# One 512-column pass for hi and lo of h, and a weight sum by transfer, in the seven-product units of a streaming encoder layer

## The chip, the cores and the metric

The kernel runs on one core of a Trainium2 chip. The metric is the device time of one execution in microseconds (us); lower is better. PE is the matrix engine (TensorE), DVE is VectorE, ACT is ScalarE, POOL is GpSimd, SP is the engine whose queue issues most transfers.

## The reference

One layer of a hybrid encoder on 512 tokens of width 2048, in float32:

```python
h = rms_norm(x, norm_gains[l, 0])
blocks = jnp.split(h @ w_in[l], 11, axis=-1)      # four head groups work on these
...
mixed = jnp.concatenate([y_sb, y_df, y_lru, y_sc], axis=-1) @ w_out[l]
x = x + rms_norm(mixed, norm_gains[l, 1])
h = rms_norm(x, norm_gains[l, 2])
x = x + rms_norm(conv_geglu_ffn(h, ffn_w_up[l], ffn_conv_w[l], ffn_w_down[l]), norm_gains[l, 3])

def conv_geglu_ffn(h, w_up, conv_w, w_down):
    u = causal_dwconv(h @ w_up, conv_w)           # 3 taps along the tokens
    g, up = jnp.split(u, 2, axis=-1)              # 4096 columns each
    return (jax.nn.gelu(g, approximate=True) * up) @ w_down
```

The change lies in `h @ w_up` and in the step between `@ w_out` and it.

## The kernel before

**Number format.** Each float32 operand of a matmul is split into two parts in PE's fast float32 format: hi (a cast on ScalarE) and lo (what is left, a subtraction on VectorE). A product is three passes: hi x hi, hi x lo and lo x hi. So each 128x128 block of weights has a hi and a lo part, and each block of h has a hi and a lo part that lie apart in one tile.

**Order.** PE's queue is in the order in which the program text issues its matmuls. Work beside the main stream of matmuls (norms, the small matmuls between) is put in by `at(block, fn)`: `tick()` counts half blocks of the stream, and `fn` is issued when its count comes. The other engines' queues are ordered at build time by a scheduler, by readiness and priority; `tc.high_priority` lifts a step, and the taps of the convolution are not lifted.

**After `@ w_out`.** The 512 tokens are worked in two halves. `residual(hf)` (line 827) normalizes the mixed result of a half, adds it to x by four accumulating transfers (POOL queue, 512 KB each, SBUF to SBUF), and books `squares` at 22, 25, 28 and 31 ticks later and `norm2` at 37 ticks later (line 838). `squares` adds up the squares of x on VectorE. `norm2` (line 854) sums them over the partitions with four small matmuls on PE (line 859), makes 1/rms, and scales and splits h. For the second half it also makes the sums of h for the units (`sums_of_h`). The matmuls of `@ w_out`, and then of the first four column tiles of `@ w_up` (`up_plain`), run on in the meantime.

**The units.** The other 28 column tiles of each half of `@ w_up` are done in 28 units (`up_unit`, line 990). A unit has four weight blocks a11, a12, a21, a22 (128 x 1024 numbers each, 512 KB) for two row halves of h and the two halves (gate and value) of the output, and computes the 2x2 block product with seven products instead of eight, from sums of blocks: s3 = a11 + a21, s1 = a21 + a22, s2 = a11 + s1, s4 = a12 + s2. s1 is added in place by an accumulating transfer from HBM on the POOL queue (in the first unit, unit 4, by VectorE); s3, s2 and s4 are added on VectorE (`add`, line 1007). s4 takes the place of a12, whose tile (`w_raw`) is the same buffer in every unit. `raw` (line 995) loads a block on the SP queue, `operand` (lines 1001 and 1002) splits one into hi and lo; three pairs of buffers go round among the operands.

`product` (line 1009) runs one of the seven: for 8 blocks k two matmuls of 256 columns with the weights' hi part (line 1021 with hi of h, line 1022 with lo of h), then 8 matmuls with the weights' lo part (line 1026), all into columns 0 to 255 of one bank. The order is 11, 21, T2, T1, T3, 22, T4; 11, T2, T3 and T4 add up in bank x, T1 and 22 in bank y, 21 is in bank w. After each, `keep` (a copy on ScalarE, line 1041) or `add_result` (an add on VectorE, line 1031) takes the bank's sum out to the tile `ub` (ug and uv in the code), and the next product into that bank waits for it. `add_rest` adds columns 256 to 511 of the bank for the products named in `JOINED`, which is empty. `conv` (lines 941 to 946) and `glu` (line 951) finish the tile, and the result goes to HBM for the down projection.

Of the kernel before, what the change touches and what calls it, by code (L numbers as in the profile page):

```python
# [12 lines left out]
ALU = mybir.AluOpType  # L13
# [3 lines left out]
P = 128  # L17
# [3 lines left out]
FF = 2 * D  # L21
EPS = 1e-6
AHEAD = 1000000

JOINED = ()
ALL = slice(0, S)
HALVES = (slice(0, S // 2), slice(S // 2, S))
NEG = -1e30
# [22 lines left out]
def trunk(ctx: ExitStack, tc: tile.TileContext, xT, params, consts, wgate, w_in, w_out, w_up0, w_up, w_dn, out):  # L51
# [722 lines left out]
    with ExitStack() as ph:  # L774
# [52 lines left out]
        def residual(hf):  # L827

            ts = HALVES[hf]
            ss1[hf].rstd(rstd1[:, ts])  # L830
            acc = ph2.tile([P, 2, S // 2], F32, name="s2")
            for q in range(4):
                for i in range(2):
                    m = mg[q][hf][:, 2 * i:2 * i + 2]
                    V.tensor_tensor(out=m, in0=m, in1=repeated(rstd1[:, ts], 2), op=ALU.mult)
                G.dma_start(out=xs[q][hf], in_=mg[q][hf], accum_op=ALU.add)
                at(clock[0] + 22 + 3 * q, lambda q=q: squares(hf, q, acc))
            at(clock[0] + 37, lambda: norm2(hf, acc))

        def squares(hf, q, acc):  # L840

# [145 lines left out]
        def by4(t):  # L987
            return flat(t).rearrange("p (a b) -> p a b", a=4)

        def up_unit(unit):  # L990
# [14 lines left out]
            def add(out, a, b):  # L1005
                with tc.high_priority(offset=AHEAD):
                    V.tensor_tensor(out=out, in0=a, in1=b, op=ALU.add)

            def product(ps, ops, name, first):


                hi, lo = ops
                kw = {} if first else {"skip_group_check": True}
                own = ps[:, 0:256]
                for k in range(8):
                    w, t = hi[:, k * P:(k + 1) * P], tops[name][k]
                    start = first and k == 0
                    if name in JOINED:
                        T.matmul(ps.rearrange("p (a t) -> p a t", a=2), lhsT=w, rhs=t, start=start, stop=False, **kw)
                    else:  # L1020
                        T.matmul(own, lhsT=w, rhs=t[:, 0], start=start, stop=False, **kw)  # L1021
                        T.matmul(own, lhsT=w, rhs=t[:, 1], start=False, stop=False, **kw)  # L1022
                    if k % 2 == 1:
                        tick()
                for k in range(8):
                    T.matmul(own, lhsT=lo[:, k * P:(k + 1) * P], rhs=tops[name][k][:, 0], start=False, stop=k == 7,  # L1026
                             **kw)

            def add_result(t, ps, *names):
                with tc.high_priority(offset=AHEAD):  # L1030
                    V.tensor_tensor(out=t, in0=t, in1=ps[:, 0:256], op=ALU.add)
                add_rest(t, ps, *names)

            def add_rest(t, ps, *names):
                if any(n in JOINED for n in names):
                    with tc.high_priority(offset=AHEAD):
                        V.tensor_tensor(out=t, in0=t, in1=ps[:, 256:512], op=ALU.add)

            def keep(t, ps, *names):
                with tc.high_priority(offset=AHEAD):  # L1040
                    A.copy(out=t, in_=ps[:, 0:256])
                add_rest(t, ps, *names)

            ug, uv = up_tile(), up_tile()
            lo_, hi_ = slice(2, 258), slice(258, 514)
# [4 lines left out]

            a11, a21 = raw(spare[n], 0, 0), raw(spare[2 + n], 1, 0)
            s3, a12, a22 = (by4(wp.tile([P, 2, S], F32, name="w_raw")) for _ in range(3))
            add(s3, a11, a21)
            s1 = a21
            if unit == 4:
                raw(a22, 1, 1)
                add(a21, a21, a22)
            else:
                with tc.high_priority(offset=AHEAD):
# [7 lines left out]
            keep(ug[:, lo_], x, "11")  # L1067
# [4 lines left out]
            add_result(ug[:, lo_], w, "21")  # L1072
            o1 = operand(s1)
            product(x, o2, "T2", False)
            keep(ug[:, hi_], x, "11", "T2")
# [4 lines left out]
            keep(uv[:, hi_], y, "T1")  # L1080
            o4 = operand(s4)
            product(x, o3, "T3", False)
            add_result(uv[:, hi_], x, "11", "T2", "T3")
            o22 = operand(a22)
            product(y, o4, "22", False)
            add_result(ug[:, hi_], y, "T1", "22")
            gate = conv(ug, 0, unit)
            product(x, o22, "T4", False)
            keep(uv[:, lo_], x, "11", "T2", "T3", "T4")
            glu(unit, gate, conv(uv, 1, unit, minus=True))  # L1090

        for unit in range(4, FF // P):
# [168 lines left out]
```

## Time and profile before

| | |
|---|---|
| median of 3 runs (range) | 1818.74 us (1817.76 to 1820.98) |
| the profiled execution | 1819.11 us |
| its span, first to last instruction | 1817.4 us |
| granted PE clock, mean over the span | 0.99 |
| PE busy | 1770.5 us, 97% of the span |
| DVE busy | 1157.0 us, 64% |
| ACT busy | 875.2 us, 48% |
| POOL busy | 103.1 us, 6% |
| moved by transfers | 256.38 MB, 141 GB/s over the span |

Busy times are sums over the span. PE's matmuls are pipelined, so their durations overlap: what one costs in a stream is read from start to start, not from its duration. A wait in a row stands in brackets: the idle time of the engine ahead of the instruction, and what ended it. The granted clock is the share of PE's full clock (2.4 GHz) that was granted; its lower level is 0.50.

### The profile page before, as it was taken

The page shows a single profiled execution, that of the slowest core. Times are in us where ns is not written, and L with a number is a line of the kernel's source. Part 1 is how long each engine was busy: PE and PEld are TensorE (multiplying, and loading weights), DVE is VectorE, ACT ScalarE, POOL GpSimd, SP SyncE. Part 2 cuts the span into 40 slices and gives each one's busy share as a digit, 9 for nine tenths or more (in the row PEclk, how much of TensorE's full clock was granted, in tenths as well). Part 3 has the DMA queues.
Part 4 walks back from the last instruction along what each step waited for, and adds up shares of the span by engine and source line. Part 5 has one row for each costly group of instructions (what it writes and reads, how often), then busy time and mean ns, then how long its engine had stood idle before and what let it go on. Part 6 is the DMA issues. An engine that isn't in the chain of part 4 may idle for free.

```text
span 1817.4 us, 27666 instructions
## 1 busy us (share of the span) xinstructions
PE 1770.5 (97%) x11180; PEld 1606.3 (88%) x11180; DVE 1157.0 (64%) x1575; ACT 875.2 (48%) x1301; POOL 103.1 (6%) x160
## 2 busy tenths in 40 slices
PE   8999999999999999899899999999999999999995
PEld 6778788887888889889899999999999988888995
DVE  7884576665666235669888887888788752222364
ACT  6442676555344334767555555554555642221342
POOL 0000111100000111100000000000000000010101
PEclk9999999999999999999999999999999999999998
DMA  7234222343332536785655455454544573323465
GB/s 255 82 104 140 75 76 83 100 126 93 93 93 93 196 117 176 230 239 167 189 148 152 140 145 153 138 141 144 156 135 128 181 248 101 97 93 102 130 207 175
DMA packets 83927, 256.38 MB, mean 141 GB/s; under 512 B 9012, under 2 KB 13364, under 8 KB 83800
## 3 DMA queue, kind: packets, MB, share of 16 engines
q1 hardware_dynamic: 78184, 235.23, 40.6%
q0 software_dynamic: 5040, 18.35, 6.1%
q8 instruction: 87, 1.43, 0.3%
q10 hardware_dynamic: 576, 1.05, 0.2%
q14 instruction: 40, 0.33, 0.1%
HBM read 230.47 MB, written 21.24 MB: 139 GB/s over the span
## 4 chain that ended last, share of the span: by engine, by line
PE 88%; DMA 4%; DVE 3%; issue 3%; ACT 2%; POOL 0%; SPq 0%; ACTq 0%; DVEq 0%; POOLq 0%
PE mm L152 39%; PE mm L1021 10%; PE mm L1022 10%; PE mm L1026 10%; PE pa L152 9%; PE mm L123 2%; PE mm L125 2%; PE mm L124 2%; PE pa L577 1%; DMA w_raw<-in_w_up_dram 1%; DMA mg<-in_w_up_dram 1%; DMA xs<-mg 1%; DMA w_raw<-in_w_out_dram 1%; DVE vd L269 1%; ACT w_hi L101 1%
## 5 line engine op out<-in xcount | busy, mean ns | idle before, releaser
L102 DVE TENSOR_TENSOR w_lo<-w_raw,w_hi 128x1024 fp32r<-128x1024 f32 (+1 forms) x249 | 305.1, 1226 | 397.2 <-PE mm L152 187.0
L101 ACT CAST w_hi<-w_raw 128x1024 fp32r<-128x1024 f32 (+1 forms) x249 | 260.6, 1047 | 444.3 <-PE mm L152 289.5
L152 PE MATMUL mm<-a,w_hi 128*128 128x512 f32 (+1 forms) x2048 | 433.1, 362 | 2.8 <-DVE t L320 2.1
L152 PEld LDWEIGHTS mm<-a,w_hi 128*128 128x128 f32 x2048 | 347.8, 190 | 61.2 <-DVE t L320 2.6
L152 PE MATMUL mm<-a,w_lo 128*128 128x512 f32 (+1 forms) x1024 | 230.8, 364 | 0.0
L1021 PE MATMUL mm<-a,w_hi 128*128 128x256 f32 x896 | 221.3, 284 | 5.1 <-ACT w_hi L1001 3.6
L1022 PE MATMUL mm<-a,w_hi 128*128 128x256 f32 x896 | 221.2, 284 | 0.0
L1001 ACT CAST w_hi<-w_raw 128x1024 fp32r<-128x1024 f32 x112 | 117.7, 1051 | 174.4 <-PE mm L1022 142.8
L152 PEld LDWEIGHTS mm<-a,w_lo 128*128 128x128 f32 x1024 | 173.1, 190 | 28.0 <-issue 1.5
L1021 PEld LDWEIGHTS mm<-a,w_hi 128*128 128x128 f32 x896 | 173.0, 193 | 5.6 <-ACT w_hi L1001 3.8
L1022 PEld LDWEIGHTS mm<-a,w_hi 128*128 128x128 f32 x896 | 173.0, 193 | 0.0
L1002 DVE TENSOR_TENSOR w_lo<-w_raw,w_hi 128x1024 fp32r<-128x1024 f32 x112 | 136.7, 1221 | 41.2 <-ACT w_hi L1001 38.7
L1026 PE MATMUL mm<-a,w_lo 128*128 128x256 f32 x896 | 126.0, 283 | 0.2 <-DVE w_lo L1002 0.2
L1001 ACT CAST w_hi<-mg 128x1024 fp32r<-128x1024 f32 x84 | 87.9, 1047 | 75.9 <-PE mm L1022 75.2
L1026 PEld LDWEIGHTS mm<-a,w_lo 128*128 128x128 f32 x896 | 115.8, 192 | 0.4 <-DVE w_lo L1002 0.4
L152 PE MATMUL pa<-a,w_hi 128*128 128x256 f32 (+1 forms) x704 | 108.5, 308 | 5.9 <-ACT w_hi L101 5.9
L1021 PE MATMUL mm<-xs,w_hi 128*128 128x256 f32 x448 | 109.9, 283 | 0.0
L1022 PE MATMUL mm<-xs,w_hi 128*128 128x256 f32 x448 | 109.9, 283 | 0.0
L152 PEld LDWEIGHTS pa<-a,w_hi 128*128 128x128 f32 x704 | 98.6, 197 | 11.7 <-ACT w_hi L101 6.6
L1002 DVE TENSOR_TENSOR w_lo<-mg,w_hi 128x1024 fp32r<-128x1024 f32 x84 | 102.4, 1219 | 3.2 <-ACT w_hi L1001 2.2
L1021 PEld LDWEIGHTS mm<-xs,w_hi 128*128 128x128 f32 x448 | 86.0, 192 | 0.0
L1022 PEld LDWEIGHTS mm<-xs,w_hi 128*128 128x128 f32 x448 | 86.0, 192 | 0.0
(273 smaller groups left out, 2730.5 us busy)
## 6 DMA issues: line engine op xcount, KB each, us to landing
w_raw<-in_w_up_dram SPq DMA_DIRECT2D x88, 512.0 KB, 5.2
w_raw<-in_w_in_dram SPq DMA_DIRECT2D x87, 512.0 KB, 3.6
w_raw<-in_w_dn_dram SPq DMA_DIRECT2D x80, 512.0 KB, 3.7
mg<-in_w_up_dram SPq DMA_DIRECT2D x56, 512.0 KB, 3.7
w_raw<-in_w_out_dram SPq DMA_DIRECT2D x48, 512.0 KB, 3.7
mg<-in_w_up_dram POOLq DMA_DIRECT2D x27, 512.0 KB, 5.8
g_d<-f SPq DMA_DIRECT2D x32, 256.0 KB, 3.0
ys<-g_d SPq DMA_DIRECT2D x32, 256.0 KB, 4.1
```

The lines of the kernel that those rows point to most:

```text
L101: w_split.append(A.copy(out=hi[:, sl], in_=raw[:, sl]))
L102: V.tensor_tensor(out=lo[:, sl], in0=raw[:, sl], in1=hi[:, sl].bitcast(F32), op=ALU.subtract)
L123: T.matmul(ps, lhsT=sh, rhs=mh, start=first, stop=False)
L124: T.matmul(ps, lhsT=sh, rhs=ml, start=False, stop=False)
L125: T.matmul(ps, lhsT=sl, rhs=mh, start=False, stop=last)
L152: T.matmul(pss[u], lhsT=a, rhs=b, start=c == 0 and kk == 0 and not low and i == 0, stop=False)
L269: V.tensor_tensor(out=ssum, in0=ssum, in1=sq, op=ALU.add)
L1001: w_split.append(A.copy(out=by4(hi), in_=v))
L1002: V.tensor_tensor(out=by4(lo), in0=v, in1=by4(hi).bitcast(F32), op=ALU.subtract)
L1021: T.matmul(own, lhsT=w, rhs=t[:, 0], start=start, stop=False, **kw)
L1022: T.matmul(own, lhsT=w, rhs=t[:, 1], start=False, stop=False, **kw)
L1026: T.matmul(own, lhsT=lo[:, k * P:(k + 1) * P], rhs=tops[name][k][:, 0], start=False, stop=k == 7, **kw)
```

## The change

- `product`: the two matmuls of 256 columns with the same weights' hi part become one of 512 columns. Its moving operand is hi and lo of a block of h, two pieces of 256 columns in one tile; its output fills the bank, hi x hi in columns 0 to 255 and hi x lo in columns 256 to 511. The 8 matmuls with the weights' lo part stay as they are.
- `add_result` and `keep`: every evacuation now also adds columns 256 to 511, with one more VectorE add of 128x256. In `keep` it comes after the copy.
- `dma_add`: s4 = a12 + s2 goes from VectorE to an accumulating transfer from SBUF to SBUF on the POOL queue, lifted in priority as that of s1.
- `residual`: `norm2` is booked 42 instead of 37 ticks later.
- `JOINED` and `add_rest` go.

```diff
-            at(clock[0] + 37, lambda: norm2(hf, acc))
+            at(clock[0] + 42, lambda: norm2(hf, acc))
...
                 for k in range(8):
-                    w, t = hi[:, k * P:(k + 1) * P], tops[name][k]
-                    start = first and k == 0
-                    if name in JOINED:
-                        T.matmul(ps.rearrange("p (a t) -> p a t", a=2), lhsT=w, rhs=t, start=start, stop=False, **kw)
-                    else:
-                        T.matmul(own, lhsT=w, rhs=t[:, 0], start=start, stop=False, **kw)
-                        T.matmul(own, lhsT=w, rhs=t[:, 1], start=False, stop=False, **kw)
+                    T.matmul(ps.rearrange("p (a t) -> p a t", a=2), lhsT=hi[:, k * P:(k + 1) * P],
+                             rhs=tops[name][k], start=first and k == 0, stop=False, **kw)
...
+            def add_result(t, ps):
                 with tc.high_priority(offset=AHEAD):
-                    V.tensor_tensor(out=t, in0=t, in1=ps[:, 0:256], op=ALU.add)
-                add_rest(t, ps, *names)
...
+                    for part in (ps[:, 0:256], ps[:, 256:512]):
+                        V.tensor_tensor(out=t, in0=t, in1=part, op=ALU.add)
+
+            def keep(t, ps):
                 with tc.high_priority(offset=AHEAD):
                     A.copy(out=t, in_=ps[:, 0:256])
-                add_rest(t, ps, *names)
+                    V.tensor_tensor(out=t, in0=t, in1=ps[:, 256:512], op=ALU.add)
+
+            def dma_add(out, in_):
+                with tc.high_priority(offset=AHEAD):
+                    G.dma_start(out=out, in_=in_, accum_op=ALU.add)
...
-                with tc.high_priority(offset=AHEAD):
-                    G.dma_start(out=a21, in_=by4(src[1, 1]), accum_op=ALU.add)
+                dma_add(a21, by4(src[1, 1]))
...
-            add(a12, a12, s2)
+            dma_add(a12, s2)
             s4 = a12
```

## Rows read from the trace of the kernel before

**Rows 1.** The page's chain that ended last, shares of the span by engine

```profile
PE 88%; DMA 4%; DVE 3%; issue 3%; ACT 2%; POOL 0%; SPq 0%; ACTq 0%; DVEq 0%; POOLq 0%
```

**Rows 2.** Busy us (instructions) of PE, PEld, DVE, ACT, POOL; clock, DMA share, GB/s

```profile
800.00:850.00 50.00, 48.15 (x383) 47.84 (x384) 46.82 (x54) 37.79 (x59) 0.00 (x0) 0.97 0.66 211
...
1100.00:1150.00 50.00, 50.00 (x419) 50.00 (x419) 42.30 (x54) 26.59 (x37) 1.98 (x3) 1.00 0.50 143
1150.00:1200.00 50.00, 50.00 (x419) 50.00 (x418) 39.24 (x48) 25.01 (x33) 2.38 (x3) 1.00 0.54 148
```

**Rows 3.** PE in order of time, in a unit: start us, us, instruction

```profile
1100.18 0.28 PE L1021 MATMUL mm<-a,w_hi 128*128 128x256 f32 x1
...
1102.10 1.12 PE L1026 MATMUL mm<-a,w_lo 128*128 128x256 f32 x8
...
1103.06 0.28 PE L1021 MATMUL mm<-a,w_hi 128*128 128x256 f32 x1
```

**Rows 4.** PE in order of time, down projection, 512 columns

```profile
1448.37 3.79 PE L152 MATMUL mm<-a,w_hi 128*128 128x512 f32 x16
1452.00 1.98 PE L152 MATMUL mm<-a,w_lo 128*128 128x512 f32 x8
```

**Rows 5.** DVE in order of time, in the unit of rows 3

```profile
1100.20 1.22 DVE L1007 TENSOR_TENSOR w_raw<-w_raw,mg 128x1024 f32<-128x1024 f32 x1
...
1107.99 1.23 DVE L1007 TENSOR_TENSOR w_raw<-mg 128x1024 f32<-128x1024 f32 x1
1109.14 1.23 DVE L1002 TENSOR_TENSOR w_lo<-w_raw,w_hi 128x1024 fp32r<-128x1024 f32 x1
...
1114.85 0.42 DVE L1031 TENSOR_TENSOR ub<-ub,mm 128x256 f32<-128x256 f32 x1 [1.61 <-PE mm L1026]
...
1118.17 1.23 DVE L1002 TENSOR_TENSOR w_lo<-w_raw,w_hi 128x1024 fp32r<-128x1024 f32 x1
```

**Rows 6.** ACT in order of time, in the same unit

```profile
1108.06 1.05 ACT L1001 CAST w_hi<-w_raw 128x1024 fp32r<-128x1024 f32 x1 [1.82 <-PE mm L1022]
1109.02 0.37 ACT L1041 COPY ub<-mm 128x256 f32<-128x256 f32 x1
...
1117.09 1.05 ACT L1001 CAST w_hi<-w_raw 128x1024 fp32r<-128x1024 f32 x1 [2.22 <-DMA w_raw<-in_w_up_dram]
```

**Rows 7.** The page's DMA issues: count, KB each, median us to landing

```profile
mg<-in_w_up_dram POOLq DMA_DIRECT2D x27, 512.0 KB, 5.8
...
xs<-mg POOLq DMA_DIRECT2D x8, 512.0 KB, 8.6
```

**Rows 8.** POOL and SP in order of time, in the same unit

```profile
1109.62 0.88 POOL L1060 DMA_DIRECT2D mg<-in_w_up_dram  x1 [19.46 <-DVE w_raw L1007]
...
1110.40 3.21 SPq L995 DMA_DIRECT2D w_raw<-in_w_up_dram  x2
```

**Rows 9.** PE and DVE in order of time, at the two norm2 steps

```profile
745.48 2.39 PE L152 MATMUL pa<-a,w_hi 128*128 128x256 f32 x16 [0.29 <-ACT w_hi L101]
751.34 1.13 PE L859 MATMUL mm<-s,con 128*128 128x256 f32 x4 [3.47 <-DVE s L848]
752.12 1.70 PE L152 MATMUL pa<-a,w_lo 128*128 128x256 f32 x8
753.62 3.21 PE L152 MATMUL pa<-a,w_hi 128*128 128x256 f32 x16
...
750.60 0.68 DVE L848 TENSOR_TENSOR s<-s,f 128x512 f32<-128x512 f32 x1
...
808.38 1.13 PE L859 MATMUL mm<-s,con 128*128 128x256 f32 x4 [1.74 <-DVE s L848]
```

**Rows 10.** PE in order of time, in the first two units

```profile
877.39 0.39 PE L1021 MATMUL mm<-a,w_hi 128*128 128x256 f32 x1 [3.58 <-ACT w_hi L1001]
...
902.75 0.42 PE L1021 MATMUL mm<-a,w_hi 128*128 128x256 f32 x1 [1.57 <-ACT ub L1041]
```

More of the change, by code (lines that the diff above doesn't have):

```diff
@@ L23 @@
 AHEAD = 1000000
-JOINED = ()
 ALL = slice(0, S)
@@ L1013, in product @@
                 kw = {} if first else {"skip_group_check": True}
-                own = ps[:, 0:256]
                 for k in range(8):
-                    w, t = hi[:, k * P:(k + 1) * P], tops[name][k]
-                    start = first and k == 0
-                    if name in JOINED:
-                        T.matmul(ps.rearrange("p (a t) -> p a t", a=2), lhsT=w, rhs=t, start=start, stop=False, **kw)
-                    else:
-                        T.matmul(own, lhsT=w, rhs=t[:, 0], start=start, stop=False, **kw)
-                        T.matmul(own, lhsT=w, rhs=t[:, 1], start=False, stop=False, **kw)
+                    T.matmul(ps.rearrange("p (a t) -> p a t", a=2), lhsT=hi[:, k * P:(k + 1) * P],
+                             rhs=tops[name][k], start=first and k == 0, stop=False, **kw)
                     if k % 2 == 1:
@@ L1025, in product @@
                 for k in range(8):
-                    T.matmul(own, lhsT=lo[:, k * P:(k + 1) * P], rhs=tops[name][k][:, 0], start=False, stop=k == 7,
-                             **kw)
-            def add_result(t, ps, *names):
+                    T.matmul(ps[:, 0:256], lhsT=lo[:, k * P:(k + 1) * P], rhs=tops[name][k][:, 0], start=False,
+                             stop=k == 7, **kw)
+            def add_result(t, ps):
                 with tc.high_priority(offset=AHEAD):
-                    V.tensor_tensor(out=t, in0=t, in1=ps[:, 0:256], op=ALU.add)
-                add_rest(t, ps, *names)
-            def add_rest(t, ps, *names):
-                if any(n in JOINED for n in names):
-                    with tc.high_priority(offset=AHEAD):
-                        V.tensor_tensor(out=t, in0=t, in1=ps[:, 256:512], op=ALU.add)
-            def keep(t, ps, *names):
+                    for part in (ps[:, 0:256], ps[:, 256:512]):
+                        V.tensor_tensor(out=t, in0=t, in1=part, op=ALU.add)
+            def keep(t, ps):
                 with tc.high_priority(offset=AHEAD):
                     A.copy(out=t, in_=ps[:, 0:256])
-                add_rest(t, ps, *names)
+                    V.tensor_tensor(out=t, in0=t, in1=ps[:, 256:512], op=ALU.add)
+            def dma_add(out, in_):
+                with tc.high_priority(offset=AHEAD):
+                    G.dma_start(out=out, in_=in_, accum_op=ALU.add)
             ug, uv = up_tile(), up_tile()
@@ L1052, in up_unit @@
             s3, a12, a22 = (by4(wp.tile([P, 2, S], F32, name="w_raw")) for _ in range(3))
+            s1 = a21
             add(s3, a11, a21)
-            s1 = a21
             if unit == 4:
@@ L1058, in up_unit @@
             else:
-                with tc.high_priority(offset=AHEAD):
-                    G.dma_start(out=a21, in_=by4(src[1, 1]), accum_op=ALU.add)
+                dma_add(a21, by4(src[1, 1]))
             raw(a12, 0, 1)
@@ L1066, in up_unit @@
             product(x, o11, "11", True)
-            keep(ug[:, lo_], x, "11")
+            keep(ug[:, lo_], x)
             o2 = operand(s2)
-            add(a12, a12, s2)
+            dma_add(a12, s2)
             s4 = a12
             product(w, o12, "21", True)
-            add_result(ug[:, lo_], w, "21")
+            add_result(ug[:, lo_], w)
             o1 = operand(s1)
             product(x, o2, "T2", False)
-            keep(ug[:, hi_], x, "11", "T2")
+            keep(ug[:, hi_], x)
             if unit > 4:
@@ L1079, in up_unit @@
             product(y, o1, "T1", True)
-            keep(uv[:, hi_], y, "T1")
+            keep(uv[:, hi_], y)
             o4 = operand(s4)
             product(x, o3, "T3", False)
-            add_result(uv[:, hi_], x, "11", "T2", "T3")
+            add_result(uv[:, hi_], x)
             o22 = operand(a22)
             product(y, o4, "22", False)
-            add_result(ug[:, hi_], y, "T1", "22")
+            add_result(ug[:, hi_], y)
             gate = conv(ug, 0, unit)
             product(x, o22, "T4", False)
-            keep(uv[:, lo_], x, "11", "T2", "T3", "T4")
+            keep(uv[:, lo_], x)
             glu(unit, gate, conv(uv, 1, unit, minus=True))
```

## The prediction

> **What bounds the kernel now.** I read the chain that ended last first: 88% of it is PE [rows 1], so time is won where PE's own instructions get shorter or where PE stands still. Next the busy time by stretches, for the stage that the diff touches, the 28 seven-product units [rows 2]: in two stretches of it PE is busy 50.00 of 50 us at a granted clock of 1.00 (2.4 GHz), VectorE 42.30 and 39.24, the DMA engines about half. The units are bound by PE, with VectorE next. Then PE in order of time [rows 3]: a product starts at 1100.18, its lo pass at 1102.10, the next product at 1103.06. That is 24 matmuls of 256 columns in 2.88 us, 0.1200 us from start to start, and 7 x 2.88 = 20.16 us a unit, without a gap. Last, the places where PE does stand: the two `norm2` steps ahead of the units [rows 9] and the first two units [rows 10].
>
> **The joined pass.** Of the 24 matmuls of a product, 16 (hi and lo of h, each against the weights' hi part) become 8 of 512 columns; the 8 of the lo pass stay. The trace has 512-column matmuls in the same number format in the stage behind the units: 16 of them from 1448.37 to 1452.00 [rows 4], 3.63/16 = 0.2269 us. Two of 256 columns take 0.2400, so a pair saves 0.0131 us. 28 units x 7 products x 8 pairs = 1568 pairs: **-20.6 us**. A product becomes 8 x 0.2269 + 8 x 0.1200 = 2.775 us, a unit 19.42. One thing has no row: the new moving operand comes in two pieces of 256 columns that lie apart, all those of before in one. If the break costs nothing it is 0.2269; if it costs what a second instruction costs it is 0.2400 and the gain is zero. I take the first, since the row has the same width and output, and keep zero as an end.
>
> The rows speak of a fixed 13 ns for each matmul on top of its columns (0.1200 against 256/2.4 = 0.1067 us). The Trainium skill, "TensorE: Matmul & The Clock Gate", section "Back-to-back issue gap", gives N/2.4 + 2.5 ns for a warm matmul, which would make a pair save some 2.5 ns and the whole, as an estimate from that page, 4 us. The rows contradict it for both widths, and the sum goes by the rows.
>
> **What the joined pass adds on VectorE.** The result now lies in both halves of the bank, so each of the seven evacuations gets one more VectorE add of 128x256: 0.42 us at 1114.85 [rows 5]. One 128x1024 add, a12 += s2, leaves VectorE: 1.22 us at 1100.20 [rows 5]. Per unit 7 x 0.42 - 1.22 = +1.7 us. VectorE now works (42.30 + 39.24)/100 x 20.16 = 16.4 us a unit; it would work 18.2 of 19.42. It fits, and the idle time in which VectorE today waits for PE (1.61 us at 1114.85) is where low-priority work (the taps and the product with the gate) can go. So I cost it at nothing, under PE as its cover. If the cover is gone, all of it is 28 x 1.7 = 48 us.
>
> What is late next is the release of bank x. Four products accumulate in it with a single other product between, and the next one may start only when both halves have been read, the second behind ScalarE's copy on which its add depends. The tightest case is T2: the copy runs at 1109.02 for 0.37 us [rows 6], VectorE is then in a subtraction of 1.23 us that began at 1109.14 [rows 5], and the add would end near 1110.37 + 0.42 = 1110.8. T3 starts four products after 1100.18, at 1111.70. The margin is 0.9 us, 0.8 with the shorter products. Behind the waiting add stand the other VectorE steps of the unit: the subtractions that make the lo operands, needed only two products later, and the taps.
>
> **The weight sum by transfer.** a12 += s2 moves to the POOL queue as an accumulating transfer of 512 KB, SBUF to SBUF. POOL has one transfer a unit today, so nothing there is pushed back; it waits for the subtraction that makes o12 and for s2, with nothing behind it on POOL until the next unit's s1. What it costs lies in a ring, because a12 uses one buffer in every unit. The next a12 is loaded (1110.40 [rows 8]) when o4 is split, and reaches its cast at 1117.09 [rows 6]: 6.7 us. Cast and subtraction end at 1119.40 [rows 5]: 2.3. Then POOL: its transfer of s1 started at 1109.62 [rows 8], 0.4 us behind the add that it needed (1107.99 for 1.23, [rows 5]); then landing, T; then cast and subtraction of o4, 1108.06 to 1110.37 [rows 5, 6]: 2.3. The ring takes 11.7 us + T and must stay under 19.42, so T under 7.7. The nearest rows: 5.8 us for the POOL sums from HBM, same size and same units, and 8.6 us for SBUF to SBUF, issued four in a row in the `residual` step [rows 7]. I take 5.8, as the new transfer runs by itself in a stage where the DMA engines are half idle [rows 2]. The ring is then 17.5 us and hidden; with 8.6 it would be 20.3 and set the pace.
>
> VectorE now works beside POOL's transfer nearly all the time. The row shows POOL's issue of s1 at 1109.62 taking 0.88 us [rows 8] while VectorE ran a subtraction with both inputs in SBUF (1109.14, [rows 5]), no longer subtraction and no stretched issue. The Trainium skill, "SBUF — State Buffer", section "Who interferes with whom", has VectorE with two SBUF inputs contend with GpSimd's reads, and calls a starved software transfer the sign of it. By the page an issue could wait out one such instruction, an estimate of 1.2 us on T, which would still leave the ring at 18.7; the trace here shows no such wait.
>
> **`norm2` five steps later.** PE's queue is written by hand, and at both `norm2` steps PE comes too early for VectorE's sum. At the first, PE ended a hi pass at 745.48 + 2.39 = 747.87 and stood until 751.34: 3.47 us. The sum was ready at 750.60 + 0.68 = 751.28. After the wait the clock was at its lower level: 24 matmuls ran at some 0.19 us (8 in 1.50, then 16 in 3.21), where at full clock they need 0.96 and 2.08: 1.67 us lost. At the second, PE stood 1.74 us [rows 9]. Five ticks later are, in this part of the queue, 4 + 4 + 8 + 8 + 4 = 28 matmuls of 0.12, or 3.36 us: the first wait goes almost whole and the clock with it, the second goes whole. 3.47 + 1.67 + 1.74: **-6.9 us**. Part is given back. Behind the second `norm2` VectorE makes the operands of the units, and is dense (46.82 of 50 us, [rows 2]). That chain starts 5.1 us earlier by the first step but 3.36 - 1.74 = 1.6 later by its own, 3.5 in all, while PE comes 6.9 earlier. If the chain sets when the units start, **+3.4**; if its slack takes that up, 0. I take 3.4 and keep both ends.
>
> **Start and end of the units.** PE waits 3.58 and 1.57 us in the first two units [rows 10] for loads that do not get faster with PE; as PE's unit is 0.7 us shorter, I put **+0.7** there, between 0 and 2 x 0.74 with the further transfer beside those loads. Behind the last product one add of 0.42 us and the last conv come before the down projection needs them only at its end: nothing.
>
> **Sum.** The profiled execution took 1819.1 us (span 1817.4), 0.4 over the median of the runs. 1819.1 - 20.6 - 6.9 + 3.4 + 0.7 = 1795.7; with the 0.4 off, 1795.
>
> **Rivals.**
> *Bank release late.* The order on VectorE is fixed when the program is built. If one more step of 1.22 us stands ahead of an add, the 0.8 us of margin become a wait of 0.4 us, once or twice a unit, perhaps with a taps' step too. 28 x 0.4 to 1.1 = 11 to 31 us: 1806 to 1826, likeliest 1807. For it: VectorE at 18.2 of 19.42. Against: these adds have high priority, the taps have not. 0.18.
> *The ring sets the pace: slower.* If the new transfer lands like those in a burst and meets the loads, T some 9.8 us, the ring is 21.5 a unit: 28 x 1.4 = +38, less 3 from `norm2`: 1854. It decides from T = 7.7 on, and turns to slower from T = 8.6 (20.3 us a unit). For it: the SBUF rows. Against: four at once there, one here. 0.06.
> *The join does nothing.* Two pieces cost as much as two matmuls: 1819 - 3 = 1816 or, with the few ns of the page named above, 1812. 0.06.
>
> **How the numbers follow.** Forecast 0.70, with its own range 1790 (all of 6.9 kept, nothing given back: 1791, and the scatter) to 1802. The rivals' share reaches up, so the range is 1790 to 1811; beyond lie the ring and the worse half of the bank case. A measurement of this kernel tells some 0.2%, 3.6 us, from no change. Faster: 0.70 + 0.13 of the bank case + 0.03 of the join = 0.86. Same: 0.03 of the bank case + 0.03 of the join + 0.01 of the ring = 0.07. Slower: 0.02 + 0.05 = 0.07.
>
> **What would show it.** In the changed profile: hi passes of 512 columns 0.227 us apart and products of 2.78 us; no wait of PE at `norm2`; VectorE at 90 to 95% in the units with PE still at 50.00 of 50; no wait of PE for an add into `ub` after the first two units; the new transfer landing in under 7.7 us. Wrong would be: products 2.88 apart, or gaps before T2, T3, 22 or T4 released by VectorE, or casts of o4 released by a transfer.

## The result, and the profile after

| kernel | median us (lowest to highest, runs) | span of the profiled execution |
|---|---|---|
| before | 1818.25 (1815.29 to 1820.98, 4) | 1817.4 |
| after | 1807.39 (1805.76 to 1809.31, 4) | 1804.7 |

The ratio is 0.9941, interval 0.9922 to 0.996: the change brought 10.9 us, where the forecast's sum had 23.4. The page of the kernel after, its busy times, the chain that ended last by engine (answers to [rows 1]) and the two transfers of the POOL queue in a unit (answers to [rows 7]: count, KB each, median us to landing):

```profile
PE 1754.3 (97%) x9612; PEld 1523.8 (84%) x9612; DVE 1182.2 (66%) x1743; ACT 869.3 (48%) x1301; POOL 127.8 (7%) x188
...
PE 90%; DMA 3%; issue 3%; DVE 2%; ACT 1%; POOL 0%; SPq 0%; POOLq 0%; ACTq 0%; DVEq 0%
...
w_raw<-mg POOLq DMA_DIRECT2D x28, 512.0 KB, 4.6
mg<-in_w_up_dram POOLq DMA_DIRECT2D x27, 512.0 KB, 5.4
```

Busy time by stretches of the kernel after, as in [rows 2], in the middle of the stage and at its start:

```profile
1100.00:1150.00 50.00, 50.00 (x288) 43.96 (x287) 44.96 (x69) 26.32 (x37) 4.38 (x5) 1.00 0.64 169
850.00:900.00 50.00, 36.74 (x224) 33.26 (x223) 40.40 (x58) 23.34 (x31) 1.74 (x2) 0.86 0.60 191
```

In the middle of the stage PE is as forecast, 50.00 of 50 at full clock, and VectorE at 44.96 a little below (from 1000 to 1400 us it is 353.45 of 400, 88%). In the 50 us around the start of the units PE is busy for 36.74 only, at a clock of 0.86. PE in order of time, first inside a unit (answers to [rows 3]), then in the first unit (answers to [rows 10]):

```profile
1100.62 2.00 PE L1013 MATMUL mm<-a,w_hi 128*128 128x512 f32 x8
1102.46 1.11 PE L1018 MATMUL mm<-a,w_lo 128*128 128x256 f32 x8
1103.41 2.00 PE L1013 MATMUL mm<-a,w_hi 128*128 128x512 f32 x8
```

```profile
864.80 2.00 PE L1013 MATMUL mm<-a,w_hi 128*128 128x512 f32 x8
...
871.44 3.15 PE L1013 MATMUL mm<-a,w_hi 128*128 128x512 f32 x8 [3.52 <-ACT w_hi L999]
...
894.18 3.78 PE L1013 MATMUL mm<-a,w_hi 128*128 128x512 f32 x8 [9.74 <-DVE ub L1029]
897.76 1.91 PE L1018 MATMUL mm<-a,w_lo 128*128 128x256 f32 x8
```

A product takes 2.79 us, 1.84 + 0.95. In the first unit PE stands 9.74 us ahead of product 22, until VectorE has taken T1's result out of bank y (L1029). Behind the wait the clock is at its lower level (1.2 GHz): the granted clock from 894 to 899 us is 0.50, and the two passes take 3.58 and 1.70 us from start to start instead of 1.84 and 0.95, 2.5 us more.

```profile
894.00:899.00 5.00, 4.82 (x14) 4.05 (x15) 1.54 (x10) 0.96 (x1) 0.00 (x0) 0.50 0.36 111
```

VectorE in order of time in that gap:

```profile
890.52 1.23 DVE L1005 TENSOR_TENSOR mg<-mg 128x1024 f32<-128x1024 f32 x1 [3.72 <-DMA mg<-in_w_up_dram]
891.66 0.68 DVE L949 TENSOR_TENSOR f<-f,f 128x512 f32<-128x512 f32 x1
...
893.04 0.75 DVE L941 SCALAR_TENSOR_TENSOR f<-ub,par,f 128x512 f32<-128x512 f32 x1
893.71 0.41 DVE L1029 TENSOR_TENSOR ub<-ub,mm 128x256 f32<-128x256 f32 x1
```

The add that releases the bank (893.71) is short, and ScalarE's copy, behind which it comes, had ended at 884.84. Ahead of it in VectorE's queue stands the sum s2 of the *next* unit (890.52, L1005), and that waits 3.72 us for the transfer of s1; then come leftovers of the plain part (L941, L949). Until 890.52 nothing on VectorE passes the step that waits.

The two `norm2` steps (answers to [rows 9]) hold PE for only 0.17 us, nearly as forecast:

```profile
751.44 1.13 PE L857 MATMUL mm<-s,con 128*128 128x256 f32 x4 [0.17 <-DVE s L846]
...
805.88 1.02 PE L857 MATMUL mm<-s,con 128*128 128x256 f32 x4
```

The accounts of the stage, read off PE's rows in order of time. "Start" is the first product of the units, "end" the first matmul of the down projection; "lost" is end less start less 28 units of 20.16 us (separate passes) or 19.55 (joined):

| kernel | start | end | lost |
|---|---|---|---|
| before | 870.78 | 1442.90 | 7.6 |
| after | 864.80 | 1430.23 | 18.0 |

The start came 6.0 us earlier and the units run 28 x 0.61 = 17.1 us faster, together 23.1. But 10.4 us more are lost inside the stage, and 12.7 are left of the span. All 18.0 us are lost in the first unit (37.49 us long, the second 19.55). In the kernel before, the first two units lost 3.8 us each (23.99 and 23.97 us for 20.16).

### The profile page after: what moved, and what is told of

Same layout as the page of the kernel before. It is cut to its first block, busy times and chain, and to the rows that moved or that the text cites. A ratio compares the mean times of both kernels' runs of the same rounds, so it can differ in the third digit from the quotient of the medians.

```text
span 1804.7 us, 24896 instructions
## 1 busy us (share of the span) xinstructions
PE 1754.3 (97%) x9612; PEld 1523.8 (84%) x9612; DVE 1182.2 (66%) x1743; ACT 869.3 (48%) x1301; POOL 127.8 (7%) x188
## 3 DMA queue, kind: packets, MB, share of 16 engines
q0 software_dynamic: 9072, 33.03, 10.4%
## 4 chain that ended last, share of the span: by engine, by line
PE 90%; DMA 3%; issue 3%; DVE 2%; ACT 1%; POOL 0%; SPq 0%; POOLq 0%; ACTq 0%; DVEq 0%
PE mm L150 40%; PE mm L1013 20%; PE mm L1018 10%; PE pa L150 10%; PE mm L121 2%; PE mm L123 2%; PE mm L122 2%; DMA w_raw<-in_w_up_dram 1%; PE pa L575 1%; DMA w_raw<-in_w_out_dram 1%; DMA xs<-mg 1%; PE pa L680 1%; DVE vd L267 0%; DMA mg<-in_w_up_dram 0%; PE pa L408 0%
## 5 line engine op out<-in xcount | busy, mean ns | idle before, releaser
L150 PEld LDWEIGHTS mm<-a,w_hi 128*128 128x128 f32 x2048 | 347.6, 189 | 61.1 <-DVE t L318 2.6
L1013 PE MATMUL mm<-a,w_hi 128*128 128x512 f32 x896 | 227.3, 396 | 13.3 <-DVE ub L1029 9.7
L1013 PEld LDWEIGHTS mm<-a,w_hi 128*128 128x128 f32 x896 | 162.7, 191 | 43.0 <-DVE ub L1029 9.9
L150 PEld LDWEIGHTS mm<-a,w_lo 128*128 128x128 f32 x1024 | 173.1, 190 | 28.1 <-issue 1.5
L1000 DVE TENSOR_TENSOR w_lo<-w_raw,w_hi 128x1024 fp32r<-128x1024 f32 x112 | 136.8, 1221 | 12.7 <-ACT w_hi L999 12.2
L1018 PEld LDWEIGHTS mm<-a,w_lo 128*128 128x128 f32 x896 | 123.7, 193 | 9.2 <-DVE w_lo L1000 0.3
L1013 PE MATMUL mm<-xs,w_hi 128*128 128x512 f32 x448 | 112.2, 392 | 0.0
L150 PEld LDWEIGHTS pa<-a,w_hi 128*128 128x128 f32 x704 | 97.0, 194 | 12.7 <-ACT w_hi L99 7.6
L1013 PEld LDWEIGHTS mm<-xs,w_hi 128*128 128x128 f32 x448 | 80.6, 189 | 14.4
L1024 DVE TENSOR_TENSOR ub<-ub,mm 128x256 f32<-128x256 f32 x168 | 70.0, 416 | 33.7 <-PE mm L1018 33.7
L1018 PEld LDWEIGHTS mm<-xs,w_lo 128*128 128x128 f32 x448 | 61.1, 190 | 4.4
L1018 PE MATMUL mm<-xs,w_lo 128*128 128x256 f32 x448 | 62.5, 282 | 0.0
L799 POOL TENSOR_TENSOR ss<-ss,q 128x256 f32<-128x256 f32 x49 | 38.0, 793 | 339.4 <-ACT q L795 338.6
```

The costliest lines, as they stand in the source:

```text
L150: T.matmul(pss[u], lhsT=a, rhs=b, start=c == 0 and kk == 0 and not low and i == 0, stop=False)
L799: G.tensor_tensor(out=self.acc, in0=self.first if self.n == 1 else self.acc, in1=sq, op=ALU.add)
L1000: V.tensor_tensor(out=by4(lo), in0=v, in1=by4(hi).bitcast(F32), op=ALU.subtract)
L1013: T.matmul(ps.rearrange("p (a t) -> p a t", a=2), lhsT=hi[:, k * P:(k + 1) * P], rhs=tops[name][k], start=first and k == 0, stop=False, **kw)
L1018: T.matmul(ps[:, 0:256], lhsT=lo[:, k * P:(k + 1) * P], rhs=tops[name][k][:, 0], start=False, stop=k == 7, **kw)
L1024: V.tensor_tensor(out=t, in0=t, in1=part, op=ALU.add)
```

## The experiments

The theory from the traces (A): the join, the moved sum and the later `norm2` each do what was forecast, and the loss lies in the order that VectorE was given at the first units. Rivals: the new transfer crowds the transfer of s1; the faster products meet the adds whatever their order; VectorE is too full. In the diffs below, `A` and `V` are ScalarE and VectorE, and `issue_after` sets a step behind another on its engine, without a wait.

**VectorE's order.** In the kernel after, the next unit's s2 is put behind T3's adds:

```diff
-            add(a11, a11, s1)
+            if t3_add:
+                with tc.issue_after(t3_add.pop().ins):
+                    add(a11, a11, s1)
+            else:
+                add(a11, a11, s1)
...
-            add_result(uv[:, hi_], x)
+            t3_add.append(add_result(uv[:, hi_], x))
```

`add_result` returns its last add here; `t3_add` holds that of the unit before.

> The changed kernel, with one edge in VectorE's order: the add s2 of a unit stands behind the two adds that take T3 of the unit before out of bank x. In the changed kernel s2 of unit 5 waits for the transfer that makes s1 (landed at 890.4 us), and the add that frees bank y for product 22 of unit 4 stands behind it; PE waits 9.7 us. Theory A (the order is the cause): the wait falls to about 5 us, since some taps still stand ahead of the add, less of the slow clock behind it too, and the time falls by 4 to 8 us, to some 1801. Rival B (the further transfer crowds the loads, everything is late): PE still waits 9 to 10 us there, for another operand, and the time stays within 2 us of 1807.

1801.37 us (1800.44 to 1802.65), ratio to before 0.9907 (0.9886 to 0.9927). VectorE, and PE's wait at product 22:

```profile
885.49 1.41 DVE L941 SCALAR_TENSOR_TENSOR f<-ub,par,f 128x512 f32<-128x512 f32 x2
...
888.81 0.41 DVE L1031 TENSOR_TENSOR ub<-ub,mm 128x256 f32<-128x256 f32 x1
...
892.12 1.23 DVE L1006 TENSOR_TENSOR mg<-mg 128x1024 f32<-128x1024 f32 x1 [1.99 <-DMA mg<-in_w_up_dram]
```

```profile
889.28 3.45 PE L1014 MATMUL mm<-a,w_hi 128*128 128x512 f32 x8 [5.81 <-DVE ub L926]
```

s2 waits for its transfer as before, now behind the adds, and 6.0 us are back. 5.81 us of wait are left; ahead of the add (888.81) stand the leftovers of the plain part.

**The transfer.** The kernel after with the fourth sum back on VectorE:

```diff
-            dma_add(a12, s2)
+            add(a12, a12, s2)
```

> The changed kernel with s4 = a12 + s2 back on VectorE; the joined pass and norm2 at 42 ticks stay. Theory A: s2 of unit 5 still stands ahead of the add that frees bank y in VectorE's order, so PE still waits 7 to 10 us in unit 4. Rival B: without the further transfer the loads come in time and the wait falls under 2 us, the time by some 10 us. For the worth of the transfer: VectorE then works 18.3 us of a unit of 19.55. If PE stays the bound, a unit stays at 19.55 us and the time within 3 us of 1807; if VectorE gets short, a unit grows towards 20 us and the time by 10 us or more.

1811.01 us (1808.26 to 1812.98), ratio 0.9954 (0.9941 to 0.9968). PE, and a stretch of the units:

```profile
893.16 3.78 PE L1013 MATMUL mm<-a,w_hi 128*128 128x512 f32 x8 [12.22 <-DVE ub L926]
```

```profile
1100.00:1200.00 100.00, 99.77 (x570) 87.41 (x569) 94.11 (x140) 52.51 (x74) 4.36 (x5) 1.00 0.51 148
```

The wait is there without the new transfer, and longer, so crowding is not what makes it. In the steady units VectorE at 94% lets PE stand 0.2 us in 100. The time is 3.6 us above that of the kernel after, of which the longer wait is 2.5.

**`norm2` alone.** The kernel before with `norm2` at 42 ticks:

```diff
-            at(clock[0] + 37, lambda: norm2(hf, acc))
+            at(clock[0] + 42, lambda: norm2(hf, acc))
```

> The kernel before with norm2 at 42 ticks alone. As the changed profile has it: the units start 6.0 us earlier and nothing is given back there, 1812 us. As the prediction put it: 6.9 us earlier and 3.4 given back at the first unit, 1815 us.

1819.67 us (1816.81 to 1820.98), ratio 1.0005 (0.9994 to 1.0016): nothing, which neither theory had. VectorE and PE:

```profile
889.77 1.22 DVE L1007 TENSOR_TENSOR mg<-mg 128x1024 f32<-128x1024 f32 x1 [6.39 <-DMA mg<-in_w_up_dram]
...
892.97 0.41 DVE L1031 TENSOR_TENSOR ub<-ub,mm 128x256 f32<-128x256 f32 x1
```

```profile
893.44 0.58 PE L1021 MATMUL mm<-mg,w_hi 128*128 128x256 f32 x1 [8.52 <-DVE ub L1031]
```

The units start at 864.28, 6.5 us earlier, and all of it is lost again behind s2, without any joined pass. In the kernel before, VectorE had the two the other way round:

```profile
889.33 0.41 DVE L1031 TENSOR_TENSOR ub<-ub,mm 128x256 f32<-128x256 f32 x1
...
897.22 1.23 DVE L1007 TENSOR_TENSOR mg<-mg 128x1024 f32<-128x1024 f32 x1 [5.74 <-DMA mg<-in_w_up_dram]
```

Moving `norm2` was enough for the scheduler to turn them. So my rival, that the faster products meet the adds, was not needed for the loss.

Nor was the wait free in the kernel before. Behind s2 stood VectorE's add of product 22. A step of ScalarE waited for that add, and behind this step came the copy that released bank x for T2 of the second unit. For this copy PE waited the 1.57 us of [rows 10] (VectorE, then ScalarE):

```profile
898.36 0.41 DVE L1031 TENSOR_TENSOR ub<-ub,mm 128x256 f32<-128x256 f32 x1
```

```profile
898.81 0.72 ACT L941 ACTIVATE f<-ub,par 128x512 f32<-128x512 f32 x1 [6.63 <-DVE ub L1031]
...
902.34 0.36 ACT L1041 COPY ub<-mm 128x256 f32<-128x256 f32 x1
```

The second unit lost 3.8 us by it, waits of 1.8 us and a lower clock.

**One contiguous piece.** The kernel after with the moving operand of the joined pass in one piece of 512 columns:

```diff
-                    T.matmul(ps.rearrange("p (a t) -> p a t", a=2), lhsT=hi[:, k * P:(k + 1) * P],
-                             rhs=tops[name][k], start=first and k == 0, stop=False, **kw)
+                    T.matmul(ps, lhsT=hi[:, k * P:(k + 1) * P],
+                             rhs=ones_piece[name][k], start=first and k == 0, stop=False, **kw)
```

> The changed kernel, but the joined pass reads 512 columns that lie in one piece (other columns of h or of its parts, so the products are of other numbers). Does the break between the two pieces cost PE time? If the break is the cause of 0.230 us a pass, a pass takes 0.2269 as in the down projection, a product 2.775 and a unit 19.42 us. If not, a product stays at 2.793 and a unit at 19.55 us.

1805.05 us in one run. PE in a unit:

```profile
1102.04 2.00 PE L1018 MATMUL mm<-a,w_hi 128*128 128x512 f32 x8
...
1104.84 2.00 PE L1018 MATMUL mm<-xs,w_hi 128*128 128x512 f32 x8
```

2.80 us from product to product again, and 19.55 us a unit as in the kernel after: the break between the two pieces costs nothing, and the 0.02 us by which a product exceeds 2.775 are not from it.

**The join alone.** The kernel before with all seven names joined, `norm2` at 37 ticks and the fourth sum on VectorE:

```diff
-JOINED = ()
+JOINED = ("11", "21", "22", "T1", "T2", "T3", "T4")
```

> The kernel before with the joined pass alone: norm2 stays 37 ticks behind its sums, and the sum of the fourth weight operand stays on VectorE. In the built order of this kernel VectorE's adds of the unit's product T3 stand ahead of the next unit's sum that waits for an accumulating transfer. Theory A (the join brings 17.1 us in 28 units; the wait of nearly 10 us at the first unit comes with the order that VectorE was given once norm2 was moved, not with the join): the wait is gone or stays near the 1.8 us of before, norm2 waits 3.5 us again as before, the unit takes 19.6 to 19.8 us with VectorE at 94%: 1818.3 - 17.1 + 1 to 3 = 1802 to 1805. Theory B (the faster products meet the adds whatever the order is): a wait of 8 to 12 us in the first unit again and 1811 to 1814. Theory C (VectorE at 94% is the bound with the join): PE waits in every unit and the unit takes 20 us or more: 1812 or more.

1812.31 us (1810.24 to 1816.3), ratio 0.9971 (0.9959 to 0.9982). None of the three holds as it stood. The time is 7 us over A's and lies in the ranges of B and C, but B's long wait in the first unit is gone, and C's units of 20 us or more do not come: PE stands 0.4 us in the 50 below. PE's waits in the units (in total, times, longest) and a steady stretch show VectorE all the same:

```profile
PE mm L1019 <- DVE ub L928: 4.8, 1, 4.8
PE mm L1019 <- DVE ub L1037: 3.2, 5, 1.7
```

```profile
1100.00:1150.00 50.00, 49.63 (x284) 43.46 (x283) 47.60 (x70) 26.54 (x38) 2.60 (x3) 1.00 0.46 137
```

T1's and T3's adds stand ahead of s2 here, and s2 still waits 4.20 us. What was held up behind it is worked off by a VectorE that is 95% full in a steady stretch and from 895 to 934 us nearly without a pause (38.17 of 39), and the waits go on: the longest, 4.84 us, stands in the third unit, at 934. 20.0 us are lost in the stage.

**Without the later `norm2`.** The kernel after with `norm2` at 37 ticks:

```diff
-            at(clock[0] + 42, lambda: norm2(hf, acc))
+            at(clock[0] + 37, lambda: norm2(hf, acc))
```

> The kernel after with norm2 put back to 37 ticks: joined pass and the moved sum, without the later norm2. In its built order VectorE's adds of T1 and T3 stand ahead of the next unit's sum. Theory A (as above): norm2 costs its 6 to 7 us again, the wait of 9.7 us in the first unit is gone, and the time is 1818.3 - 17.1 = 1801, within 1799 to 1803: the later norm2 costs the kernel after some 6 us instead of bringing 7. Theory B (the wait belongs to the join): wait of 8 to 12 us, time 1807.4 + 6 = 1813.

1800.42 us (1799.02 to 1803.96), ratio 0.9909 (0.9895 to 0.9922), as A said: 7.0 us faster than the kernel after, by *taking out* one of its three parts. VectorE:

```profile
886.72 0.41 DVE L1024 TENSOR_TENSOR ub<-ub,mm 128x256 f32<-128x256 f32 x1
887.05 1.22 DVE L1000 TENSOR_TENSOR w_lo<-mg,w_hi 128x1024 fp32r<-128x1024 f32 x1
888.18 0.41 DVE L1024 TENSOR_TENSOR ub<-ub,mm 128x256 f32<-128x256 f32 x1
893.23 1.23 DVE L1005 TENSOR_TENSOR mg<-mg 128x1024 f32<-128x1024 f32 x1 [4.63 <-DMA mg<-in_w_up_dram]
```

s2 waits 4.63 us, longer than the 3.72 in the kernel after, but behind both adds of T3, and PE's longest wait for VectorE is 2.7 us. The adds of T1 and T3 stand ahead of s2 as in the join alone, and the fourth sum is on a transfer: 11.9 us less. So the transfer is worth its place where VectorE has something to catch up.

**The leftovers too.** The order of the first experiment, with the plain part's last convolutions (second half, columns 1 to 3) behind the first unit's adds of T3:

```diff
+                if half == 1 and u >= 1:
+                    later.append(lambda: done(u))
+                    return None
...
             t3_add.append(add_result(uv[:, hi_], x))
+            if later:
+                with tc.issue_after(t3_add[-1].ins):
+                    while later:
+                        later.pop(0)()
```

> The kernel of the first experiment (the adds of T3 ahead of the next unit's sum) with one more change of order: the convolutions and products with the gate that are left over from the plain part (second half, columns 1 to 3) are put behind the first unit's adds of T3 on VectorE; there they stood as 3.5 us of work ahead of the add that releases the bank for which PE waited 5.8 us. Theory A (what PE waits for is VectorE's order alone): the wait falls from 5.8 to about 2 us, and the time from 1801.4 to 1797, within 1795.5 to 1798.5. Theory B (the add waits for ScalarE's copy and the transfers, and the left-over work only fills the gap): the wait stays at 5 to 6 us and the time at 1801.

1795.07 us (1793.7 to 1796.0), ratio 0.9873 (0.986 to 0.9886): the fastest of all, 12.3 us under the kernel after: 6.0 of them by s2's place, 6.3 by the leftovers'. That is theory A, 0.4 us below its range. VectorE at the same place, then PE's two waits in the units:

```profile
885.11 0.42 DVE L1030 TENSOR_TENSOR ub<-ub,mm 128x256 f32<-128x256 f32 x1 [1.11 <-PE mm L1024]
...
886.58 0.42 DVE L1030 TENSOR_TENSOR ub<-ub,mm 128x256 f32<-128x256 f32 x1
887.21 1.22 DVE L1011 TENSOR_TENSOR mg<-mg 128x1024 f32<-128x1024 f32 x1 [0.21 <-DMA mg<-in_w_up_dram]
```

```profile
872.09 3.33 PE L1019 MATMUL mm<-a,w_hi 128*128 128x512 f32 x8 [3.63 <-ACT w_hi L1005]
...
908.54 2.11 PE L1019 MATMUL mm<-mg,w_hi 128*128 128x512 f32 x8 [0.96 <-DVE ub L1030]
```

Here the adds wait for PE, not PE for the adds. From 1000 to 1400 us VectorE is busy for 351.63 of 400 (88%) and PE for all 400, so the rival that VectorE is too full is out for this kernel.

**The loads.** The kernel just shown, with the second unit's first two loads behind the first unit's four on SP:

```diff
-            a11, a21 = raw(spare[n], 0, 0), raw(spare[2 + n], 1, 0)
+            if unit == 5:
+                with tc.issue_after(w_load[-1].ins):
+                    a11, a21 = raw(spare[n], 0, 0), raw(spare[2 + n], 1, 0)
+            else:
+                a11, a21 = raw(spare[n], 0, 0), raw(spare[2 + n], 1, 0)
```

> The kernel of the run with the left-over work put later, and the two first loads of the second unit put behind the first unit's four loads in the DMA queue of SyncE. Theory A (the first unit's second product waits 2.7 us for its weights because two loads of the next unit, 512 KB each, go ahead of them): the wait at the second product falls from 2.7 us to under 0.7, and the time by 2 to 4 us more, to 1793 to 1795. Theory B (the loads share the DMA engines whatever their order is, or the second product waits for ScalarE): the wait stays and the time is that of the run before.

1797.7 us (1795.38 to 1801.98), ratio 0.9891 (0.9876 to 0.9905): not faster. The wait of 3.63 us went, to 0.96, but VectorE and PE paid in the second unit:

```profile
887.59 1.23 DVE L1011 TENSOR_TENSOR mg<-mg 128x1024 f32<-128x1024 f32 x1 [5.52 <-DMA mg<-in_w_up_dram]
```

```profile
896.85 3.78 PE L1019 MATMUL mm<-a,w_hi 128*128 128x512 f32 x8 [3.97 <-DVE ub L1036]
```

s2 of the second unit starts no earlier than in the kernel just shown (887.21): the transfer of s1 is issued 1.3 us earlier (POOL, 878.91 for 880.18) but takes 8.7 us to land instead of 6.9. So what the first unit won was lost behind s2, and neither theory had this. That the loads put back slow the transfer is likely, but not shown.

**What the later `norm2` is worth once the order is right,** asked twice: the kernel before with `norm2` at 42 ticks and both edits of order (no join, no moved sum), and the fastest kernel with `norm2` back at 37.

> The kernel before with norm2 at 42 ticks, and VectorE's order at the first units as in the fastest run so far: the next unit's sum behind the add of T3, the left-over convolutions of the plain part behind it too. No joined pass, no moved sum. Theory A (norm2 five ticks later is worth 4 to 6 us at the start of the units, and the run with that edit alone lost it again to VectorE's order): 1812 to 1815, the wait of 8.5 us in the first unit under 3. Theory B (the gain at the start is eaten by the loads and the transfer of the second unit, which come no earlier, whatever VectorE's order is): 1818 to 1820, with a wait of another name at the first two units.

> The fastest kernel so far (joined pass, moved sum, VectorE's order at the first units set by hand) with norm2 put back to 37 ticks. Theory A (norm2 late is worth 4 to 6 us once the order is right): 1795.1 + 4 to 6 = 1799 to 1801. Theory B (what the late norm2 brings is lost again at the first units): 1795 to 1796.

1812.09 us (1809.89 to 1813.99), ratio 0.9968 (0.9956 to 0.9979), so 5.7 us under the kernel before; and 1801.64 us (1797.94 to 1802.05), ratio 0.9904 (0.9889 to 0.9919), 6.6 us over the run at 42 (5.6 by the ratios). Theory A in both, in the second 0.6 us above its range. With `norm2` at 37 PE's waits there are back: two, 5.4 us in total, the longest 3.7. Only the second is a clean price of `norm2`; the 5.7 us hold the two edits of order too.

**The ring.** The kernel after with the new transfer issued twice:

```diff
             dma_add(a12, s2)
+            dma_add(a12, s2)
```

> The kernel after with the new accumulating transfer issued twice, one behind the other (so the fourth weight operand holds the sum with its second term counted twice). In the kernel after, it lands 4.6 us behind its issue, some 3.4 us before the cast that reads it. Forecast by the ring of the prediction: two in a row take 8 to 9.5 us to the second landing, the ring is at its limit and PE waits 0 to 1.5 us in a unit: 1807 to 1849. If the ring had no room, as the rival had it, the 4.6 us would come back in full in every unit: 1807 + 28 x 4.6 = 1936. If transfers beside each other crowd the loads, the second product's load lands late too and PE waits there.

1889.4 us in one run, over the forecast. POOL in a unit, and ScalarE's cast that reads the sum:

```profile
1107.56 0.87 POOL L1033 DMA_DIRECT2D w_raw<-mg  x1 [13.67 <-DVE ub L1024]
1112.68 0.86 POOL L1033 DMA_DIRECT2D w_raw<-mg  x1 [4.25 <-DMA w_raw<-mg]
```

```profile
1118.25 1.05 ACT L999 CAST w_hi<-w_raw 128x1024 fp32r<-128x1024 f32 x1 [4.26 <-DMA w_raw<-mg]
```

The second is issued only when the first has landed, so that the sum is there 10.7 us behind the first issue, not 8 to 9.5: the size that I expected for two transfers was wrong. The spans differ by (1887.7 - 1804.7)/28 = 3.0 us a unit. The units behind the first take some 20.5 and 25 us by turns, 22.8 on average, near the 11.7 + 10.7 = 22.4 of the prediction's ring. But PE does not wait for a weight there. Its waits are for VectorE's adds, 45.0 us in 34 waits, and these for ScalarE's copy, which stands behind the cast that waits for the sum; a lower clock (0.95 from 1000 to 1400 us) adds to them. VectorE's add, then PE:

```profile
1119.60 0.42 DVE L1029 TENSOR_TENSOR ub<-ub,mm 128x256 f32<-128x256 f32 x1 [2.45 <-ACT ub L1028]
```

```profile
1120.08 2.12 PE L1013 MATMUL mm<-xs,w_hi 128*128 128x512 f32 x8 [0.70 <-DVE ub L1029]
```

So 4.6 us are hidden and 10.7 are not. That the limit lies at 7.7, where the prediction had it, is not shown: no run has a transfer near it.

**The width.** The kernel after with the lo pass 512 columns wide too:

```diff
-                    T.matmul(ps[:, 0:256], lhsT=lo[:, k * P:(k + 1) * P], rhs=tops[name][k][:, 0], start=False,
-                             stop=k == 7, **kw)
+                    T.matmul(ps.rearrange("p (a t) -> p a t", a=2), lhsT=lo[:, k * P:(k + 1) * P],
+                             rhs=tops[name][k], start=False, stop=k == 7, **kw)
```

> The kernel after with the second pass of a product (lo of the weights by hi of h) also 512 columns wide, so that no pass changes width (it adds lo by lo, which the kernel leaves out, to the other half of the bank). The product takes 2.793 us in the kernel after where the sum of the prediction had 2.775. Theory A (the 0.02 us come with each change of width): the product takes 16 x 0.2269 = 3.63 us. Theory B (a joined pass is slower by itself, 0.230 a matmul): 3.68 us. The time goes up by some 28 x 7 x 0.84 = 165 us either way.

1959.73 us in one run. PE in a unit:

```profile
1100.47 1.98 PE L1013 MATMUL mm<-a,w_hi 128*128 128x512 f32 x8
1102.28 1.98 PE L1018 MATMUL mm<-a,w_lo 128*128 128x512 f32 x8
1104.09 1.98 PE L1013 MATMUL mm<-a,w_hi 128*128 128x512 f32 x8
```

A unit is 25.39 us, so a product is 3.63 us and a matmul 0.2267, as in [rows 4]. The 0.02 us come with the change of width. The time is 152 us over the kernel after and not 165, as PE waits only 5.2 us in the first unit here, for 13.3.

The stage's accounts once more, for the runs that change order and parts:

| kernel | `norm2` | start | end | lost | median us |
|---|---|---|---|---|---|
| before with later `norm2` | 42 | 864.28 | 1442.90 | 14.1 | 1819.67 |
| the same, order set | 42 | 864.27 | 1435.94 | 7.2 | 1812.09 |
| join alone | 37 | 867.28 | 1434.66 | 20.0 | 1812.31 |
| join and transfer | 37 | 866.43 | 1424.08 | 10.2 | 1800.42 |
| the same, order set | 37 | 871.81 | 1425.43 | 6.2 | 1801.64 |
| after, fourth sum on VectorE | 42 | 864.04 | 1432.65 | 21.2 | 1811.01 |
| after, s2 behind T3's adds | 42 | 864.85 | 1424.24 | 12.0 | 1801.37 |
| the same, leftovers behind too | 42 | 865.46 | 1419.82 | 7.0 | 1795.07 |
| the same, loads put back | 42 | 863.54 | 1421.45 | 10.5 | 1797.7 |

With both edits of order, and the loads as they were, the stage loses 6 to 7 us whatever else is changed, about what it lost in the kernel before (7.6). The start scatters by some us from profile to profile (866.4 to 871.8 at 37 ticks, 863.5 to 865.5 at 42 in the two tables), so the worth of `norm2` is taken from the medians.

## Why the prediction came out wrong, step by step

**The failed step: "Start and end of the units".** I put +0.7 us there, and the kernel after lost 10.4 more than the kernel before. I had read PE's waits in the first two units [rows 10] and put both down to loads. The second is none: it is a bank release behind ScalarE's copy, held up by s2 on VectorE. I did not read VectorE's queue in the same 30 us. There, in the kernel before, s2 of the second unit waited 5.74 us for its transfer; that cost PE 3.8 us, and not more, because T3's add happened to stand ahead of it. I costed `norm2` by times alone ("that chain starts 5.1 us earlier"), as if VectorE's steps kept their places. They are placed by a scheduler, the move turned two of them round, and the wait came to stand ahead of a bank release, with the leftovers behind it. Shown by the run of `norm2` alone (8.5 us, no join), by the run without it (gone), and by setting the order by hand (12.3 us back).

**The give-back: too large.** I put +3.4 us for a later start of the units behind VectorE's chain. They started 6.0 us earlier where 6.9 were on offer, so 0.9 were given back, near the end of 0 that I had kept.

**My rival "bank release late" had the mechanism, at the wrong place.** "One more step of 1.22 us ahead of an add" was to cost 0.4 to 1.1 us in every unit. In the steady units it never came; in the first unit it came once, and the step ahead was one that waits. I had worked out the margin of bank x alone; the wait of 9.74 us is at bank y, whose release after T1 is a VectorE add only since the join. Neither the forecast nor the rival looked there. That the time is the rival's likeliest, 1807, is luck.

**The joined pass: right, 17.1 us for 20.6.** The mis-sized term is the 0.2269 us: a row from a stream of one width. Between passes of 256 and 512 columns a product takes 2.793 us, not 2.775; 196 times 0.018 is the missing 3.5 us. A joined matmul costs 0.230 us there (1.84/8). By the figure that I set against the rows, the Trainium skill, "TensorE: Matmul & The Clock Gate", section "Back-to-back issue gap", the join would have brought some 4 us as an estimate; 17.1 us were measured, and the measurement decides. The section gives that figure for a single matmul by itself, not for a stream, which I had not said.

**The moved sum: right.** T was put at 5.8 us and is 4.6, and no cast waited for this transfer in the steady units. POOL's issues take 0.86 to 0.90 us there beside a VectorE that is 88% busy, so the wait of 1.2 us that I had estimated by the Trainium skill, "SBUF — State Buffer", section "Who interferes with whom", does not show. The section itself reports that a `tensor_tensor` was not seen to stall a transfer, and with that the trace agrees; I had left it out. What I had at nothing is worth more: without the transfer, with `norm2` at 37 ticks in both, the time is 11.9 us higher.

**VectorE: 88%, forecast 94.** I added seven adds at their duration of 0.42 us. In a stream such an add takes 0.33 us from its start to that of the next step (from 886.72 to 887.05 in the run without the later `norm2`). Seven of these less the 1.13 us of the sum that left (887.05 to 888.18, a step of the same size) make +1.2 us a unit instead of +1.7, or 90%; the rest I did not trace. The remark that I made for PE, that one reads from start to start, holds for VectorE too.

**`norm2`: right, 6.6 us for 6.9** (5.6 by the ratios), but only where the order is held fixed. Alone, as built, it brings nothing.

**The sum.** The fastest kernel runs in 1795.07 us, the time that was forecast for another one. That is luck, errors that cancel: the units start 5.3 us earlier (865.46 for 870.78) where I had 6.9 - 3.4 = 3.5, and lose 0.6 us less inside (7.0 for 7.6) where I had 0.7 more; these 3.1 us stand against 3.5 that the products did not gain.

What stays open: the wait of 1.7 to 4.6 us for the first unit's second operand, for which the run with the loads put back only exchanged one wait for another.

## What to carry to other kernels

Before an edit moves work in time, look along every in-order engine for the steps that wait for a transfer, and ask what stands behind each: a wait that costs little today can cost its whole length once the step that PE needs is placed behind it. Where a scheduler makes the queues, a shift of a few us can turn them round, so hold the steps that release banks ahead of those that wait, and only then judge the edit. And take the price of an instruction from start to start in a stream of the same mixture, not from a pure one.

## What the runs showed of the hardware

- A change between passes of 256 and 512 columns costs PE some 0.02 us a product (2.793 against 8 x 0.2269 + 8 x 0.1200 = 2.775 us); with all passes 512 wide a product is 16 x 0.2267. A moving operand in two pieces runs as fast as one in one piece (19.55 us a unit in both).
- After 9.74 us of standing still, PE's next 8 matmuls of 512 columns took 3.78 us and the 8 of 256 columns 1.91, against 2.00 and 1.11 at full clock (2.4 GHz); the granted clock from 894 to 899 us was 0.50, its lower level (1.2 GHz). After 0.96 us of standing still, in the fastest kernel, 8 of 512 columns took 2.11, all but full speed.
- An accumulating transfer of 512 KB from SBUF to SBUF landed in 4.6 us when issued singly in the units, against 8.6 when four are issued in a row [rows 7]. Two into the same tile took 10.7 us, the second issued when the first had landed.
- VectorE's durations overlap in a stream: an add of 128x256 is recorded with 0.41 us and takes 0.33 from start to start, a subtraction of 128x1024 with 1.22 and takes 1.13 (886.72, 887.05 and 888.18 in the run without the later `norm2`).
